# A decoder layer on one core: six weight loads in uneven parts, the last w3 in halves of its rows, and the last sums in another order

## The chip, the cores and the metric

The kernel runs on one core of a Trainium2 chip. A core has five engines with a queue of instructions each: TensorE (PE, with its weight loads shown apart as PEld), VectorE (DVE), ScalarE (ACT), GpSimd (POOL) and SyncE (SP), which here issues nearly all transfers. Sixteen DMA engines move the data between the chip's memory (HBM) and the on-chip memory of 128 partitions. Engines wait for each other and for transfers through semaphores. The metric is device microseconds of one execution, as the median of several runs.

## What is computed

The reference is one layer of a decoder for 512 tokens of width 1024, all in float32: a mixer of two kinds of attention, then a mixture of 64 experts of which each token takes two, then a final RMSNorm. The change touches the experts and the norm behind them:

```python
def expert_block(args):
    xb, e = args
    return (jax.nn.silu(xb @ w1[e]) * (xb @ w3[e])) @ w2[e]
...
x = x + hier_moe(h, w_group[l], b_group[l], w_expert[l], b_expert[l], w1[l], w3[l], w2[l])
return rms_norm(x, final_norm)
```

An expert has three matrices of 2 MB: w1 and w3 are 1024 x 512, w2 is 512 x 1024. All 64 experts' matrices are read once, 403 MB.

## The kernel before

The mixer takes the first 380 us or so. Then come the experts, in 16 batches of four (N_BATCH). Each expert has 32 places for tokens, so that a batch fills 128 rows; what doesn't fit is done after the last batch by a loop that runs as many times as a counter says (`overflow`, L1509; zero times for these inputs).

A batch runs so. The tokens of its four experts are gathered into `hsel` by matmuls with a selection matrix (g_ps, L1261). Then h1 and h3 are summed up in two accumulators (L1571): for each of eight chunks of 128 rows of the matrix, and in it for each of the four experts, one matmul of 32 columns against 512. A matmul in float32 is two instructions in the trace, so 32 matmuls per matrix stand there as 64. `swiglu` makes gg and its transpose gT, then y_ps is summed up from gT and w2 (L1608), and `combine` multiplies by the gates and adds the result to four accumulators `accs`, one for each block of 128 tokens (c_ps, L1368 and L1374). In the first batches the routing and in the fifth the row of the final norm are prepared beside it.

The weights come through a ring of eight tiles of 128 partitions x 16 KB, in three pools of 2, 4 and 2 (RING). `load_next` (L1030) takes the next entry of the list `loads`, claims the next tile and issues the transfer on SP; the tile must have been released by the matmuls that read it, so SP waits for TensorE. An entry is one expert's matrix as a whole, and the order is w1, w3, w2 with four experts each. In the last batch w2 is loaded in halves of its rows, two experts to a tile, and the second half of the rows again in column blocks (CUTS: 512, 256, 256), so that the last columns come last (`load_half`, L978).

The last batch has its own end, `last_outputs` (L1406): `values(i, chunks)` sums up y_psl for a column block, `evac(i)` copies it, `add(t, cuts)` multiplies by the gates and adds it to `accs[t]` (c_psl, L1428 and L1430), `square(t, i)` makes sums of squares on ScalarE (L1380), `final_weight` multiplies by the norm's weights on GpSimd, `final_factors` makes the reciprocal root of two blocks at a time on VectorE and GpSimd (L1388 to L1398), and `output` scales and stores. Inside it all engines run in the order of the code; in the batches before it, a scheduler orders the instructions.

Of the kernel before, what the change touches and what calls it, by code (L numbers as in the profile page):

```python
# [16 lines left out]
OP = mybir.AluOpType  # L17
# [3 lines left out]
P = 128  # L21
T = 512
NT = T // P
D = 1024
# [20 lines left out]
ANGLES_AT = 6  # L45
FORGET_AT = 13
ROUNDS = (5, 3)

CUTS = ((0, 512), (512, 768), (768, 1024))
BIG = 3e38  # L50
EPS = 1e-6
# [45 lines left out]
def kernel(ctx: ExitStack, tc: tile.TileContext, a: dict, out: bass.AP, dbg=None):  # L97
# [860 lines left out]
    loads = [[(0, m, k, e) for m, k, e in halves[n_first:n_first + 2]], [(0, m, k, e) for m, k, e in halves[n_first + 2:]]]  # L958
    for b in range(1, N_BATCH - 1):
        loads += [[(b, m, None, e)] for m in ("w1", "w3", "w2") for e in range(4)]  # L960
    loads += [[(N_BATCH - 1, m, None, e)] for m in ("w1", "w3") for e in range(4)]
    loads += [[(N_BATCH - 1, "w2", k, e + u) for u in range(2)] for k in range(2) for e in (0, 2)]
    next_places = [0] * RING[0] + [1] * RING[1] + [2] * RING[2]

    def weights(m, x, k):

        w, n = {"w1": (w1, NC), "w3": (w3, NC), "w2": (w2, 4)}[m]
        rows = w[x].rearrange("(p c) n -> p c n", c=n)
        return rows if k is None else rows[:, k * n // 2:(k + 1) * n // 2]
# [60 lines left out]
    def load_next():  # L1030

        i = len(issued) - n_first
        issued.append(i)
        t = rings[next_places[i % n_ring]].tile([P, 4096], F32, tag="ring", name=f"load{i}")
        if len(loads[i]) == 1 and loads[i][0][2] is None:
            b, m, k, e = loads[i][0]
            t = t.rearrange("p (c n) -> p c n", c=4 if m == "w2" else NC)
            nc.sync.dma_start(t, weights(m, 4 * b + e, k))  # L1038
            note(b, m, k, e, [t[:, c] for c in range(t.shape[1])])
            return  # L1040
        for u, x in enumerate(loads[i]):
            load_half(t[:, 2048 * u:2048 * u + 2048], *x)
# [335 lines left out]
    def square(t, i):  # L1378

        act.activation(gg.rearrange("p c n -> p (c n)")[:, 0:512], accs[t][:, rest_cut if i else first_cut], AF.Square,  # L1380
                       accum_out=sq4[:, t, i:i + 1])

    def final_weight(t):
        gp.tensor_tensor(outs[t][:, first_cut], accs[t][:, first_cut], fnorm[:, first_cut], op=OP.mult)
# [3 lines left out]
    def final_factors(t, n=2):  # L1388

        q, ms, r, e = (r4[:, j, t:t + n] for j in range(4))  # L1390
        v.tensor_tensor(ms, sq4[:, t:t + n, 0], sq4[:, t:t + n, 1], op=OP.add)
        v.tensor_scalar(ms, ms, 1.0 / D, EPS, op0=OP.mult, op1=OP.add)
        gp.tensor_tensor(r, ms, mhalf[:, 0:n], op=OP.pow)
        yield
        v.tensor_tensor(e, r, r, op=OP.mult)
        v.tensor_tensor(e, e, ms, op=OP.mult)
        v.tensor_scalar(e, e, -0.5, 1.5, op0=OP.mult, op1=OP.add)
        v.tensor_tensor(r, r, e, op=OP.mult)  # L1398

    def output(t):  # L1400
        r, o = r4[:, 2, t:t + 1], outs[t]
# [4 lines left out]
    def last_outputs():  # L1406

        y_ps = [o_tile(f"y_psl{i}") for i in range(2)]
        y_ps = [y_ps[0], y_ps[1][:, 0:256], s_tile("y_psl2")[:, 0:256]]
        y_sb = [ys[0], ys[1][:, 0:256], ys[1][:, 256:512]]  # L1410

        def values(i, chunks):
            for c in chunks:
                for e in range(4):
                    q = slice(32 * e, 32 * e + 32)
                    w = last[i, c][e] if c > 1 else wt[N_BATCH - 1, "w2", e][c][:, slice(*CUTS[i])]
                    pe.matmul(y_ps[i][q], gT[:, c, q], w, start=c == 0, stop=c == 3, skip_group_check=True)

        def evac(i):
            act.activation(y_sb[i], y_ps[i], AF.Copy)  # L1420

        def add(t, cuts):

            c_ps = (acc_tile if t < 2 else pt_tile)(f"c_psl{cuts[0]}_{t}")
            s = slice(CUTS[cuts[0]][0], CUTS[cuts[-1]][1])
            for i in cuts:
                a0, a1 = (x - s.start for x in CUTS[i])
                pe.matmul(c_ps[:, a0:a1], w_t[:, t], y_sb[i], start=i == cuts[0], stop=i == cuts[-1],  # L1428
                          skip_group_check=True)
            v.tensor_tensor(accs[t][:, s], c_ps, accs[t][:, s], op=OP.add)  # L1430


        for i in range(3):
            values(i, range(2))
        values(0, range(2, 4))
        evac(0)
        for t in range(2):
            add(t, (0,))
            final_weight(t)
        for t in range(2):  # L1440
            square(t, 0)
        values(1, range(2, 4))
        evac(1)
        for t in range(2, NT):
            add(t, (0,))
            final_weight(t)
        square(2, 0)
        values(2, range(2, 4))
        evac(2)
        square(3, 0)  # L1450

        f = [final_factors(t) for t in (0, 2)]
        for t in range(NT):
            add(t, (1, 2))
            square(t, 1)
            if t == 2:
                next(f[0])
        next(f[0], None)
        next(f[1])
        output(0)  # L1460
        output(1)
        next(f[1], None)
        output(2)
        output(3)

    def prepare_overflow():

        cnt = flat[7][:, 0:5 * N_EXP].rearrange("p (j e) -> p j e", j=5)
        c_n, n_blk, inc, one64, c_t = (cnt[:, j] for j in range(5))
        cnt_ps = o_tile("cnt_ps")  # L1470
        for u in range(NT):
            pe.matmul(cnt_ps[:, 0:N_EXP], ones_b, picks[:, u], start=u == 0, stop=u == NT - 1)
        v.tensor_copy(c_n, cnt_ps[:, 0:N_EXP])
        v.tensor_scalar(n_blk, c_n, float(CAP), None, op0=OP.is_gt)
        for j in range(1, 4):
            v.tensor_scalar(c_t, c_n, float(CAP + P * j), None, op0=OP.is_gt)
            v.tensor_tensor(n_blk, n_blk, c_t, op=OP.add)
        v.memset(one64, 1.0)
        v.tensor_tensor_scan(inc, one64, n_blk, 0.0, op0=OP.mult, op1=OP.add)
        v.tensor_tensor(c_t, inc, n_blk, op=OP.subtract)  # L1480
        ovs = moe.tile([P, 2, NT], F32, name="ovs")
        over = moe.tile([P, 2, NT], F32, name="over")
        val = scr[:, 0:512].rearrange("p (x t e) -> p x t e", x=2, t=NT)
        for x in range(2):
            v.tensor_tensor(val[:, x], oh[:, x], c_t[:, None, :].to_broadcast([P, NT, N_EXP]), op=OP.mult)
        v.tensor_reduce(ovs, val, axis=AX.X, op=OP.add)
        for t in range(NT):
            v.tensor_copy(exs[:, :, t], topi[:, t, 8:10])
        v.scalar_tensor_tensor(poss, exs, -float(CODE), slots, op0=OP.mult, op1=OP.add)

        v.scalar_tensor_tensor(ovs, ovs, float(P), poss, op0=OP.mult, op1=OP.add)
        v.tensor_scalar(over, poss, float(CAP), None, op0=OP.is_ge)  # L1492
        v.scalar_tensor_tensor(ovs, ovs, 1.0 - CAP, over, op0=OP.add, op1=OP.mult)
        v.tensor_scalar(ovs, ovs, -1.0, None, op0=OP.add)
        ov_row = moe.tile([1, NB_MAX + 1], F32, name="ov_row")
        ov_int = moe.tile([1, NB_MAX + 1], I32, name="ov_int")
        done = scr[0:1].rearrange("o (i e) -> o i e", e=N_EXP)
        for k in range(2):
            v.tensor_tensor(done, inc[0:1, None, :].to_broadcast([1, 16, N_EXP]),
                            iota[0:1, 16 * k:16 * k + 16, None].to_broadcast([1, 16, N_EXP]), op=OP.is_le)  # L1500
            v.tensor_reduce(ov_row[:, 16 * k:16 * k + 16], done, axis=AX.X, op=OP.add)
        v.tensor_scalar(ov_row[:, 0:NB_MAX], ov_row[:, 0:NB_MAX], float(N_EXP - 1), None, op0=OP.min)
        v.tensor_copy(ov_row[:, NB_MAX:NB_MAX + 1], inc[0:1, N_EXP - 1:N_EXP])
        v.tensor_copy(ov_int, ov_row)
        nxt = moe.tile([1, NB_MAX], I32, name="nxt")
        n_ov = nc.values_load(ov_int[0:1, NB_MAX:NB_MAX + 1], min_val=0, max_val=NB_MAX)
        return ovs, ov_int, nxt, n_ov

    def overflow(ovs, ov_int, nxt, n_ov):  # L1509
        ov_w = [u.rearrange("p (c n) -> p c n", c=2) for u in flat[7:9]]  # L1510
        ov_loads = []
        with tc.For_i(0, n_ov):
# [28 lines left out]
            for t in range(NT):  # L1541
                for i in range(2):
                    square(t, i)
                final_weight(t)
            for _ in final_factors(0, NT):
                pass
            for t in range(NT):
# [5 lines left out]
    def load_ahead(n):  # L1553
        while len(issued) - n_first < min(n, len(loads)):
            load_next()
# [3 lines left out]
    loc = slots  # L1559

    for b in range(N_BATCH):
        load_ahead(2 + 12 * b + n_ring if b else RING[0] + RING[1])
        h1, h3 = s_tile(f"h1_{b}"), s_tile(f"h3_{b}")

# [62 lines left out]
                pe.matmul(f_ps, one_row, row[:, 512 * k:512 * k + 512], start=True, stop=True)  # L1627
                act.activation(fnorm[:, 512 * k:512 * k + 512], f_ps, AF.Copy)

    overflow(*ov)  # L1630


# [24 lines left out]
```

## Time and profile before

| | us |
|---|---|
| median of 3 runs (1313.0 to 1313.3) | 1313.22 |
| the profiled execution | 1313.3 |
| its span, first to last instruction | 1311.3 |
| TensorE busy | 1126.6 |
| VectorE busy | 457.5 |
| ScalarE busy | 245.7 |
| GpSimd busy | 73.6 |

The page cuts the span in 40 slices of 32.8 us. A digit is the busy share of a slice in tenths, and below it stand the GB/s that the DMA engines moved. The mixer fills the first 11 or 12 slices, the experts the rest. PEclk, or the granted clock, is the share of TensorE's full clock of 2.4 GHz that it was given: 1.0 or 0.5 (1.2 GHz) at any moment. A busy TensorE isn't one at its peak, since matmuls are pipelined.

### The profile page before, as it was taken

The page shows a single profiled execution, that of the slowest core. Times are in us where ns is not written, and L with a number is a line of the kernel's source. Part 1 is how long each engine was busy: PE and PEld are TensorE (multiplying, and loading weights), DVE is VectorE, ACT ScalarE, POOL GpSimd, SP SyncE. Part 2 cuts the span into 40 slices and gives each one's busy share as a digit, 9 for nine tenths or more (in the row PEclk, how much of TensorE's full clock was granted, in tenths as well). Part 3 has the DMA queues.
Part 4 walks back from the last instruction along what each step waited for, and adds up shares of the span by engine and source line. Part 5 has one row for each costly group of instructions (what it writes and reads, how often), then busy time and mean ns, then how long its engine had stood idle before and what let it go on. Part 6 is the DMA issues. An engine that isn't in the chain of part 4 may idle for free.

```text
span 1311.3 us, 16877 instructions
## 1 busy us (share of the span) xinstructions
PE 1126.6 (86%) x6934; PEld 610.5 (47%) x6934; DVE 457.5 (35%) x1138; ACT 245.7 (19%) x559; POOL 73.6 (6%) x100
## 2 busy tenths in 40 slices
PE   8999999999999797978879696968878786967865
PEld 8987777878984262413233241413232331413212
DVE  7776666236263362212303121212313121211113
ACT  5665444433541000000000000000000000000003
POOL 2700000012000000000000000000000000000002
PEclk9999999999999899979989898989889998989878
DMA  5222231356989999999999999999999999999995
GB/s 185 76 66 74 78 88 55 96 146 202 347 280 417 427 427 426 428 427 428 427 426 428 427 427 426 428 426 428 428 426 427 421 428 424 428 426 427 428 421 190
DMA packets 70074, 438.92 MB, mean 335 GB/s; under 512 B 9878, under 2 KB 39594, under 8 KB 45036
## 3 DMA queue, kind: packets, MB, share of 16 engines
q1 hardware_dynamic: 69994, 437.82, 82.3%
q8 instruction: 56, 0.92, 0.3%
q14 instruction: 22, 0.18, 0.0%
q10 hardware_dynamic: 2, 0.00, 0.0%
HBM read 433.48 MB, written 2.10 MB: 332 GB/s over the span
## 4 chain that ended last, share of the span: by engine, by line
PE 63%; DMA 31%; DVE 3%; SPq 1%; issue 1%; ACT 1%; POOL 1%; DVEq 0%; POOLq 0%; ACTq 0%
DMA load<-in_w_dram 30%; PE h L1571 11%; PE y_ps L1608 9%; PE g_ps L1261 9%; PE c_ps L1368 8%; PE acc_g L322 2%; PE acc_g L323 2%; PE acc_g L324 2%; SPq L1038 1%; PE of_ps L823 1%; PE acc_wo L324 1%; PE acc_kv L433 1%; PE acc_wo L322 1%; PE acc_wo L323 1%; PE fpT_ps L805 1%
## 5 line engine op out<-in xcount | busy, mean ns | idle before, releaser
L1571 PE MATMUL h<-load,u_hi 128*32 128x512 f32 x1920 | 293.3, 671 | 88.3 <-DMA load<-in_w_dram 88.1
L1608 PE MATMUL y_ps<-load,u_hi 128*32 128x512 f32 x920 | 167.9, 680 | 53.6 <-DMA load<-in_w_dram 50.3
L1571 PEld LDWEIGHTS h<-load,u_hi 128*32 128x32 f32 x1920 | 69.6, 121 | 288.4 <-issue 155.9
L1261 PEld LDWEIGHTS g_ps<-u_hi,xc 128*128 128x128 f32 x1024 | 118.8, 194 | 24.6 <-issue 13.0
L1261 PE MATMUL g_ps<-u_hi,xc 128*128 128x128 f32 x1024 | 124.9, 281 | 0.6 <-DVE over L1492 0.6
L1374 DVE TENSOR_TENSOR u_lo<-c_ps,u_lo 128x512 f32<-128x512 f32 x84 | 58.1, 692 | 188.3 <-PE c_ps L1368 188.3
L1608 PEld LDWEIGHTS y_ps<-load,u_hi 128*32 128x32 f32 x920 | 40.5, 117 | 168.8 <-issue 89.3
L1267 DVE TENSOR_TENSOR u_hi<-g_ps,cst 128x512 f32<-128x512 f32 (+1 forms) x33 | 21.9, 667 | 278.1 <-PE h L1571 261.5
L1368 PE MATMUL c_ps<-xb,xb 128*128 128x512 f32 x240 | 116.7, 617 | 1.0 <-DVE u_lo L1371 0.8
L1355 ACT ACTIVATE xb<-h 128x512 f32<-128x512 f32 x16 | 9.6, 597 | 355.9 <-PE h L1571 355.9
L1368 PEld LDWEIGHTS c_ps<-xb,xb 128*128 128x128 f32 x240 | 37.8, 188 | 79.4 <-DVE u_lo L1374 36.8
L1343 POOL TENSOR_TENSOR xb<-xb,u_hi 128x512 f32<-128x512 f32 x16 | 20.4, 1273 | 824.8 <-DVE xb L1342 748.4
L1365 ACT ACTIVATE xb<-y_ps 128x512 f32<-128x512 f32 x30 | 17.9, 597 | 216.4 <-PE y_ps L1608 216.4
L1362 ACT ACTIVATE u_hi<-t_ps 128x512 f32<-128x512 f32 x16 | 9.6, 597 | 255.3 <-PE t_ps L1361 255.3
L322 PE MATMUL acc_g<-hT_hi,hi_g 128*128 128x512 f32 x128 | 54.2, 423 | 0.0
L1211 DVE TENSOR_SCALAR u_hi<-codes,locs,cst 128x128 f32<-128x128 f32 x60 | 21.8, 363 | 87.5 <-PE g_ps L1261 87.5
L323 PE MATMUL acc_g<-hT_lo,hi_g 128*128 128x512 f32 x128 | 50.5, 395 | 0.0
L324 PE MATMUL acc_g<-hT_hi,lo_g 128*128 128x512 f32 x128 | 50.4, 394 | 0.0
L1356 DVE TENSOR_TENSOR u_hi<-h,xb 128x512 f32<-128x512 f32 x16 | 16.5, 1033 | 90.0 <-PE h L1571 89.1
L189 DVE TENSOR_TENSOR lo_g<-raw_g,hi_g 128x1024 fp32r<-128x1024 f32 x16 | 19.6, 1226 | 36.1 <-ACT hi_g L187 36.1
L322 PE MATMUL acc_wo<-hi_wo,mT 128*128 128x256 f32 x96 | 28.7, 299 | 0.0
L324 PE MATMUL acc_wo<-hi_wo,mT 128*128 128x256 f32 x96 | 27.1, 283 | 0.1
(377 smaller groups left out, 1604.3 us busy)
## 6 DMA issues: line engine op xcount, KB each, us to landing
load<-in_w_dram SPq DMA_DIRECT2D x176, 2048.0 KB
first<-in_w_dram SPq DMA_DIRECT2D x16, 1024.0 KB
load<-in_w_dram SPq DMA_DIRECT2D x9, 1024.0 KB
raw_g<-in_w_in_dram SPq DMA_DIRECT2D x16, 512.0 KB
raw_wo<-in_w_out_dram SPq DMA_DIRECT2D x8, 512.0 KB
x_sb<-in_x_dram SPq DMA_DIRECT2D x4, 512.0 KB
raw_qs<-in_w_in_dram SPq DMA_DIRECT2D x4, 512.0 KB
raw_vf<-in_w_in_dram SPq DMA_DIRECT2D x4, 512.0 KB
```

The costliest lines, as they stand in the source:

```text
L189: defer(wait, lambda: v.tensor_tensor(lo, r, hi.bitcast(F32), op=OP.subtract))
L322: pe.matmul(o, l_hi, r_hi, start=first, stop=False, skip_group_check=True)
L323: pe.matmul(o, l_hi, r_lo, start=False, stop=False, skip_group_check=True)
L324: pe.matmul(o, l_lo, r_hi, start=False, stop=last, skip_group_check=True)
L1211: v.tensor_scalar(sel1[:, t], labels, loc[:, 0, t:t + 1], r, op0=OP.is_equal, op1=OP.mult)
L1261: pe.matmul(g_ps[k][:, c * P:(c + 1) * P], xc[t][:, 4 * k + c], sel1[:, t], start=(t, c) == (0, 0), stop=t == NT - 1, skip_group_check=True)
L1267: v.tensor_tensor(hsel[:, d], g_ps[k][:, c * P:(c + step) * P].rearrange("p (c n) -> p c n", c=step), g_ffn[:, d, None].to_broadcast([P, s ...
L1343: gp.tensor_tensor(wsel, wsel, wtmp, op=OP.add)
L1368: pe.matmul(c_ps, w_t[:, t], ys[k], start=True, stop=True)
L1374: v.tensor_tensor(d, c_ps, d, op=OP.add)
L1571: pe.matmul(o[s], hsel[:, c, s], wt[b, m, e][c], start=c == 0, stop=c == NC - 1, skip_group_check=True)
L1608: pe.matmul(y_ps[k][s], gT[:, c, s], wt[b, "w2", e][c][:, 512 * k:512 * k + 512], start=c == 0, stop=c == 3, skip_group_check=True)
```

## The change

Four things change. Line numbers move by up to nine; the words below name functions.

First, six entries of `loads`, the third expert's w1 in batches 1, 4, 6, 9, 11 and 14, are issued as three transfers: partitions 0 to 111, 112 to 119 and 120 to 127. Second, the last batch's w3 is loaded as its w2 was: the first half of the rows of experts 0 and 1, then of 2 and 3, then the second halves. Third, in `last_outputs` all four `add(t, (0,))` come before the two later column blocks of y_psl, and the mean of squares is built as one operation for each pair of blocks from a term that is made once for all four. Fourth, the counter of the overflow loop is read into the engines' registers at the start of the last batch and not in batch 1.

```diff
+UNEVEN = [(b, "w1", 2) for b in (1, 4, 6, 9, 11, 14)]
...
-    loads += [[(N_BATCH - 1, m, None, e)] for m in ("w1", "w3") for e in range(4)]
-    loads += [[(N_BATCH - 1, "w2", k, e + u) for u in range(2)] for k in range(2) for e in (0, 2)]
+    loads += [[(N_BATCH - 1, "w1", None, e)] for e in range(4)]
+
+    loads += [[(N_BATCH - 1, m, k, e + u) for u in range(2)] for m in ("w3", "w2") for k in range(2) for e in (0, 2)]
...
-            nc.sync.dma_start(t, weights(m, 4 * b + e, k))
+            src = weights(m, 4 * b + e, k)
+
+            for p0, p1 in ((0, 112), (112, 120), (120, 128)) if (b, m, e) in UNEVEN else ((0, P),):
+                nc.sync.dma_start(t[p0:p1], src[p0:p1])
...
-        v.tensor_tensor(ms, sq4[:, t:t + n, 0], sq4[:, t:t + n, 1], op=OP.add)
-        v.tensor_scalar(ms, ms, 1.0 / D, EPS, op0=OP.mult, op1=OP.add)
+        v.scalar_tensor_tensor(ms, sq4[:, t:t + n, 1], 1.0 / D, q, op0=OP.mult, op1=OP.add)
...
+    def first_sums():
+
+        v.tensor_scalar(r4[:, 0], sq4[:, :, 0], 1.0 / D, EPS, op0=OP.mult, op1=OP.add)
...
-        for t in range(2):
+        for t in range(NT):
             add(t, (0,))
             final_weight(t)
-        for t in range(2):
-            square(t, 0)
-        values(1, range(2, 4))
-        evac(1)
-        for t in range(2, NT):
-            add(t, (0,))
-            final_weight(t)
-        square(2, 0)
-        values(2, range(2, 4))
-        evac(2)
+            if t < 3:
+                square(t, 0)
+        for i in (1, 2):
+            values(i, range(2, 4))
+            evac(i)
         square(3, 0)
...
+            if t == 0:
+                first_sums()
...
+        if b == N_BATCH - 1:
+            with tc.manual_schedule(engines={E.PE, E.DVE, E.Activation, E.Pool, E.SP}):
+                n_ov = nc.values_load(ov[1][0:1, NB_MAX:NB_MAX + 1], min_val=0, max_val=NB_MAX)
```

SP's queue at the loads of batch 1, before and after. A row is a line of the kernel, the transfer, the tile that it fills and that tile's shape (partitions x elements).

```order
126 L1038 DMA load_4226<-in_w_dram 128x4096
127 L1038 DMA load_4228<-in_w_dram 128x4096
128 L1038 DMA load_4230<-in_w_dram 128x4096
129 L1038 DMA load_4232<-in_w_dram 128x4096
130 L1038 DMA load_4392<-in_w_dram 128x4096
```

```order
126 L1044 DMA load_4226<-in_w_dram 128x4096
127 L1044 DMA load_4228<-in_w_dram 128x4096
128 L1044 DMA load_4230<-in_w_dram 112x4096
129 L1044 DMA load_4230<-in_w_dram 8x4096 x2
130 L1044 DMA load_4234<-in_w_dram 128x4096
```

The third load of the batch became three transfers into the same tile, one behind the other, ahead of the fourth.

TensorE at the last batch's w3, before and after: h_15 with the higher number is the accumulator of h3. Of before four tiles take turns, one for each expert, for all eight chunks; the first rows stand here.

```order
3797 L1571 MATMUL h_15_7629<-load_7407,u_hi_3867 32x512
3798 L1571 MATMUL h_15_7630<-load_7409,u_hi_3867 32x512
3799 L1571 MATMUL h_15_7630<-load_7411,u_hi_3867 32x512
3800 L1571 MATMUL h_15_7630<-load_7413,u_hi_3867 32x512
3801 L1571 MATMUL h_15_7630<-load_7415,u_hi_3867 32x512
```

```order
3799 L1580 MATMUL h_15_7649<-load_7407,u_hi_3867 32x512 x2
3800 L1580 MATMUL h_15_7649<-load_7410,u_hi_3867 32x512 x2
3801 L1580 MATMUL h_15_7649<-load_7413,u_hi_3867 32x512 x2
3802 L1580 MATMUL h_15_7649<-load_7416,u_hi_3867 32x512 x2
3803 L1580 MATMUL h_15_7649<-load_7413,u_hi_3867 32x512 x2
```

The first four chunks now read only the first two tiles (7407 and 7410, the first halves of all four experts' rows), and the last four only the other two; before, each chunk read all four tiles.

TensorE at the end, before and after: y_psl are the three column blocks of the last product, c_psl their sums with the gates.

```order
3844 L1417 MATMUL y_psl_7720<-load_7621,u_hi_3868 32x512 x8
3845 L1428 MATMUL c_psl_0_7756<-xb_3060,xb_3061 128x512
3846 L1428 MATMUL c_psl_1_7760<-xb_3060,xb_3061 128x512
3847 L1417 MATMUL y_psl_7721<-load_7624,u_hi_3868 32x256 x8
3848 L1428 MATMUL c_psl_2_7775<-xb_3060,xb_3061 128x512
3849 L1428 MATMUL c_psl_3_7779<-xb_3060,xb_3061 128x512
3850 L1417 MATMUL y_psl_7722<-load_7624,u_hi_3868 32x256 x8
```

```order
3823 L1426 MATMUL y_psl_7739<-load_7640,u_hi_3868 32x512 x8
3824 L1437 MATMUL c_psl_0_7775<-xb_3060,xb_3061 128x512
3825 L1437 MATMUL c_psl_1_7780<-xb_3060,xb_3061 128x512
3826 L1437 MATMUL c_psl_2_7785<-xb_3060,xb_3061 128x512
3827 L1437 MATMUL c_psl_3_7790<-xb_3060,xb_3061 128x512
3828 L1426 MATMUL y_psl_7740<-load_7643,u_hi_3868 32x256 x8
3829 L1426 MATMUL y_psl_7741<-load_7643,u_hi_3868 32x256 x8
```

The second column block moved behind the third and fourth sums of the first, and stands next to the third block.

## Rows read from the trace of the kernel before

**Rows 1.** The page: busy time of engines; DMA share and GB/s by slice

```profile
PE 1126.6 (86%) x6934; PEld 610.5 (47%) x6934; DVE 457.5 (35%) x1138; ACT 245.7 (19%) x559; POOL 73.6 (6%) x100
...
DMA  5222231356989999999999999999999999999995
GB/s 185 76 66 74 78 88 55 96 146 202 347 280 417 427 427 426 428 427 428 427 426 428 427 427 426 428 426 428 428 426 427 421 428 424 428 426 427 428 421 190
```

**Rows 2.** Chain that ended last: start us, us, what; its shortest and longest load wait

```profile
498.94 22.78 DMA load<-in_w_dram
...
1242.46 29.92 DMA load<-in_w_dram
```

**Rows 3.** One stretch: its length, engines' busy us (instructions), granted clock, DMA share, GB/s

```profile
400.00:1260.00 860.00, 703.06 (x4182) 272.76 (x4178) 210.97 (x499) 44.56 (x77) 20.37 (x16) 0.92 1.01 427
```

**Rows 4.** The page's DMA parts: queue, packets, MB, share; an issue and its size

```profile
q8 instruction: 56, 0.92, 0.3%
...
load<-in_w_dram SPq DMA_DIRECT2D x176, 2048.0 KB
```

**Rows 5.** Stretches of 1 us at the end of the last loads, columns as above

```profile
1288.00:1289.00 1.00, 1.00 (x16) 0.33 (x12) 0.00 (x0) 0.00 (x0) 0.00 (x0) 1.00 0.87 291
1289.00:1290.00 1.00, 0.83 (x8) 0.00 (x0) 0.00 (x0) 0.10 (x1) 0.00 (x0) 1.00 0.56 194
1290.00:1291.00 1.00, 0.45 (x1) 0.30 (x2) 0.00 (x0) 0.50 (x1) 0.00 (x0) 1.00 0.46 159
1291.00:1292.00 1.00, 1.00 (x4) 0.38 (x2) 0.29 (x1) 0.00 (x0) 0.00 (x0) 1.00 0.24 83
1292.00:1293.00 1.00, 1.00 (x14) 0.36 (x16) 0.83 (x2) 0.56 (x2) 0.46 (x1) 1.00 0.06 19
```

**Rows 6.** Stretches of 1 us during a load of w_proj_fox and two of w_proj_swa

```profile
257.00:258.00 1.00, 1.00 (x6) 0.79 (x5) 0.74 (x1) 0.23 (x1) 0.00 (x0) 1.00 0.72 253
...
298.00:299.00 1.00, 1.00 (x6) 0.79 (x5) 0.33 (x2) 0.00 (x0) 0.00 (x0) 1.00 1.19 209
299.00:300.00 1.00, 1.00 (x6) 0.82 (x5) 0.67 (x1) 0.00 (x0) 0.26 (x1) 1.00 1.13 219
```

**Rows 7.** Timeline of the issues of these loads: start us, us, queue, line, transfer

```profile
254.92 0.37 SPq L174 DMA_DIRECT2D raw_pf<-in_w_proj_fox_dram  x1
...
295.23 1.27 SPq L174 DMA_DIRECT2D raw_ps<-in_w_proj_swa_dram  x2
```

**Rows 8.** Timeline of TensorE at the last w3; in brackets idle time before, and what ended it

```profile
1267.61 1.91 PE L1571 MATMUL h<-load,u_hi 128*32 128x512 f32 x2 [3.97 <-DMA load<-in_w_dram]
...
1272.42 9.52 PE L1571 MATMUL h<-load,u_hi 128*32 128x512 f32 x58 [2.91 <-DMA load<-in_w_dram]
...
1274.13 0.20 PEld L1571 LDWEIGHTS h<-load,u_hi 128*32 128x32 f32 x4 [0.66 <-issue]
...
1278.35 0.12 PEld L1571 LDWEIGHTS h<-load,u_hi 128*32 128x32 f32 x4 [0.31 <-issue]
```

**Rows 9.** Two stretches of 5 us during the last w3, columns as in rows 3

```profile
1272.00:1277.00 5.00, 4.58 (x24) 1.18 (x28) 0.00 (x0) 0.00 (x0) 0.00 (x0) 0.50 1.01 417
1277.00:1282.00 5.00, 4.94 (x38) 1.06 (x30) 0.00 (x0) 0.00 (x0) 0.00 (x0) 0.96 1.02 390
```

**Rows 10.** Timeline of the end: last group of y_psl, a sum, and two small operations

```profile
1295.38 1.07 PE L1417 MATMUL y_psl<-load,u_hi 128*32 128x256 f32 x16
...
1298.55 0.69 DVE L1430 TENSOR_TENSOR u_lo<-c_psl,u_lo 128x512 f32<-128x512 f32 x1 [0.17 <-PE c_psl L1428]
...
1300.09 0.16 DVE L1391 TENSOR_TENSOR r<-sq 128x2 f32<-128x2 f32 x1
...
1300.29 0.17 DVE L1392 TENSOR_SCALAR r<-r 128x2 f32<-128x2 f32 x1
```

**Rows 11.** SP's waits: queue, line, for whom; us in total, times, longest

```profile
SPq L1038 <- PE h L1571: 497.4, 37, 22.4
...
SPq L994 <- PE h L1571: 26.4, 3, 17.9
```

More of the change, by code (lines that the diff above doesn't have):

```diff
@@ L1505, in prepare_overflow @@
         nxt = moe.tile([1, NB_MAX], I32, name="nxt")
-        n_ov = nc.values_load(ov_int[0:1, NB_MAX:NB_MAX + 1], min_val=0, max_val=NB_MAX)
-        return ovs, ov_int, nxt, n_ov
+        return ovs, ov_int, nxt
     def overflow(ovs, ov_int, nxt, n_ov):
@@ L1544, in overflow @@
                 final_weight(t)
+            first_sums()
             for _ in final_factors(0, NT):
@@ L1628 @@
                 act.activation(fnorm[:, 512 * k:512 * k + 512], f_ps, AF.Copy)
-    overflow(*ov)
+    overflow(*ov, n_ov)
 _INS = ["x", "positions", "attn_norm", "w_in", "b_forget", "b_gate", "attn_sinks", "w_proj_fox",
```

## The prediction, made before the changed kernel had run

> **What bounds the kernel now.** I read the busy table first, then the slices, then the chain of waits, and last the two places that the change touches. TensorE is busy 86% of the span, but from the twelfth slice on the DMA row stands at 9 and the bytes at 417 to 430 GB/s with hardly a break [rows 1]. Over the 860 us from 400 to 1260 the sixteen DMA engines are busy all the time (share 1.01) and move 427 GB/s [rows 3]. The chain confirms that this stage is the loads' own: each batch of four experts ends in a wait of 22 to 30 us for a weight load before TensorE goes on [rows 2]. So a microsecond of TensorE inside a batch is worth nothing, and a microsecond of a DMA engine counts, if that engine is one that finishes last. Only behind the last load does TensorE's own work set the end.
>
> A load is 2048 KB [rows 4], 128 rows of 16 KB; at 427 GB/s it takes 4.9 us, and an engine moves a row of 16 KB in 0.61 us (427/16 = 26.7 GB/s). The engines don't stop together: the share falls from 0.87 through 0.46 to 0.06 between 1288 and 1293 [rows 5]. Summed, they stop 2.8 us before 1293 on average, half of them by about 1290, so half have some 3 us to spare. A cause is at hand: 56 instruction fetches of 16 KB ride on the same engines [rows 4], and they need not fall evenly.
>
> **The change, part by part.** The profiled execution took 1313.3 us with a span of 1311.3; the median of the three runs is 1313.22, so the sum is made on 1313.3 and needs no correction.
>
> *Six loads in 112, 8 and 8 rows.* The bytes stay the same. With a row to an engine, 112 rows are seven for each of sixteen, and each piece of 8 is one row for eight engines. If both pieces go to the same eight, these move nine rows for such a load and the others seven: over six loads 6 x 0.61 = 3.7 us more on eight engines and 3.7 us less on the others. If the eight are the early half, this evens out what the share row shows.
>
> The price of a piece is what the trace doesn't show. Its lower end is 0.61 us, a row at the usual rate. But few partitions are slow in this trace: the load of w_proj_fox, which fills 128 partitions, moves 253 GB/s at a share of 0.72, which is 351 GB/s of busy engines, while the loads of w_proj_swa, of 64 partitions each, run with all engines busy at 209 and 219 GB/s [rows 6, 7]. The engines are not short of work there, each byte only takes 351/214 = 1.64 times as long. If a piece of 8 partitions is no worse than that, its row takes 0.61 x 1.64 = 1.0 us. If the rate goes on falling with the partitions, 8 of 128 get 1/16 of 427 GB/s, and the 128 KB of a piece take 4.9 us. I take 2.2 us, the middle of 1.0 and 4.9 by ratio: the step from 128 to 64 cost less than in proportion, and eight partitions go much further down than 64. Twelve pieces then cost 12 x (2.2 - 0.61) = 19.1 us on the engines that carry them. The whole range is 0 (lower end) to 12 x 4.3 = 51.5 us. An engine that waits in a piece gets nothing back later, since what is queued behind it, the next load, runs at the full rate anyway.
>
> The SBUF page of the Trainium skill ("SBUF — State Buffer", Door 1: The DMA port swizzle) has a rule that speaks against this part. It says that four neighbouring partitions share one of sixteen ports, and gives 27.6 GB/s for partitions 0 to 3. By it partitions 112 to 119 lie on two ports, a piece takes an estimated 2.4 us, and the sum below would be 1332.8. The trace agrees in direction (64 partitions at 0.61 of the rate); eight partitions no row here shows. Its DMA page ("DMA: Bandwidth & Descriptors", Why a DMA increments its semaphore by 16 and not by 1) would send an 8-partition copy to the eight lowest-numbered engines; no row shows engine numbers.
>
> Twelve more issues on SP cost nothing: SP stands 497 us waiting for TensorE before such loads [rows 11]. That wait is the cover; without it they would cost about 0.4 us each.
>
> *The last w3 in halves of its rows.* Today TensorE does a few matmuls of w3 early, the last 2 of these at 1267.6, and 58 of 64 only after 1272.42, when the fourth expert's load is in: 9.5 us, its first 5 us at a granted clock of 0.50 and the rest near 1.0 [rows 8, 9]. In the new order the first half of the rows of all four experts is multiplied before the last piece lands, and 28 of 64 stay. In the trace 4 weight loads with their matmuls follow each other in 0.86 us at the low level (1.2 GHz) and in 0.43 at the high one (2.4) [rows 8], so 28 take 3.0 to 6.0 us, and the gain ahead of the SwiGLU is 3.5 to 6.5 us. It can't all reach the end: the last bytes of w2 land shortly before 1293 [rows 5], and today the last 16 matmuls on them start at 1295.38 [rows 10]. So at most 2.4 us come out of the wait, then the landing is late next. I book 2.4.
>
> *The order of the last sums.* All four first sums stand before the last two groups of y_psl, which then run back to back. That fits the landing just named and costs nothing while TensorE waits there; ACT takes three squares before the second copy, covered by the same wait. On VectorE two operations of 0.16 and 0.17 us become one, twice [rows 10]; one of the two places lies on the path, with a bit of the other: 0.3 us. The added operation on all four sums falls in the gap of 0.17 us that VectorE has ahead of its sums [rows 10].
>
> *The register load of the overflow count* goes from batch 1, where SP waited for it, to the last batch. There it stands ahead of a wait of up to 17.9 us for h [rows 11], so it is hidden; where it stood it cost nothing, since the engines were full (share 1.01 [rows 3]). Zero. In batches 4, 6, 9, 11 and 14 TensorE also takes one group of matmuls a little later; the wait for loads hides that.
>
> **Sum.** Pieces +19.1, extra rows on the eight engines +3.7, their spare time -3.0, the end -2.4 - 0.3: +17.1 us, 1330.4. With a piece at 1.0 us it is +2.7 (1316), at 4.9 us +49.5 (1363).
>
> **The rivals.**
> *Pieces at the usual rate.* The eight engines are spread over 3 us, so they may not meet at the same partitions, and the rows are large. Then the loads end 0 to 2.2 us earlier (2.2 is perfect evenness, the sum of the shares in [rows 5]); with 1.5 us and the end's 2.7 the time is 1309.1. This is the case on the other side, and it decides for faster as soon as a piece stays under about 0.8 us, since 12 x 0.2 = 2.4 is about what the evening and the end give. Against it stands the row of 64 partitions.
> *The pieces meet the late half.* At the usual rate, but on engines that finish last: +3.7 - 2.7, 1314.3, within what can be told. Or the rows are halved with no gain at the end: 1312 to 1313.
>
> **How the numbers follow.** Slow pieces 0.56, by the only rows that show few partitions. Usual rate 0.36, because no row has pieces of 16 KB rows on eight engines. The late half or no gain 0.08. The range goes from 1306, a bit below the fast rival, to 1346, which takes a piece at up to 3.6 us; slow pieces alone would be 1316 to 1363. A change of 0.2% (2.6 us) is about what a measurement of this kernel tells from none. Faster by more than that 0.38 (the fast rival and a little of the third), within 0.06, slower 0.56.
>
> **What would show it.** If the pieces are slow, the bytes in 20 us around each of the six loads fall from 427 GB/s by a twentieth or more, waits of TensorE for loads grow in batches 1, 4, 6, 9, 11 and 14, and the first multiplication of w3's last batch comes 15 us or more later. If they aren't, the steady stage stays at 427 GB/s, and the DMA share before the last landing stays near 1 and then drops within 1 or 2 us. In both cases fewer than 30 matmuls of w3 should follow the last w3 landing, and the last group of y_psl should start right at w2's landing. I am wrong if the six batches show no more wait than the others, or if the end doesn't close up by 2 us.

## The result: 4.45% slower

The changed kernel took 1372.16 us in the median (1367.8 to 1374.9), the kernel before 1313.0 beside it: a ratio of 1.0445, 95% interval 1.0431 to 1.0459. That is 59 us more, where the prediction said 17. The direction was right; the time lies above the range.

The page of the changed kernel, the parts that answer to [rows 1]:

```profile
PE 1141.1 (83%) x6934; PEld 613.2 (45%) x6934; DVE 457.2 (33%) x1137; ACT 246.1 (18%) x559; POOL 73.5 (5%) x100
...
DMA  6223232375899999999999999999999999999994
GB/s 186 63 63 94 72 85 61 93 232 196 311 370 345 427 425 427 426 346 427 428 426 307 428 426 427 397 330 421 427 420 331 421 418 387 425 377 365 424 409 160
```

TensorE runs as many instructions as before (6934). The DMA row stands at 9 from the thirteenth slice to the last but one, as before, but in six places the bytes fall (345, 346, 307, 330, 331 and 365 GB/s at their lowest): the engines don't run out of work, their work takes longer. Stretches of 20 us around the third of these places, batch 6 (columns as in rows 3; the last two are the DMA share and GB/s):

```profile
700.00:720.00 20.00, 16.90 (x125) 5.04 (x125) 6.48 (x20) 1.69 (x3) 1.28 (x1) 0.91 1.03 426
720.00:740.00 20.00, 18.04 (x87) 10.13 (x85) 6.91 (x12) 1.19 (x2) 0.00 (x0) 1.00 0.99 222
740.00:760.00 20.00, 11.03 (x65) 2.55 (x66) 0.00 (x0) 0.60 (x1) 0.00 (x0) 0.79 1.01 428
```

For 20 us everything moves at half speed, with a share of 0.99, and then all is well again. Two whole loads' bytes pass in this time, though only one load is in parts. In stretches of 1 us:

```profile
718.00:719.00 1.00, 1.00 (x16) 0.36 (x9) 0.00 (x0) 0.00 (x0) 0.00 (x0) 1.00 0.81 344
719.00:720.00 1.00, 1.00 (x10) 0.23 (x3) 0.00 (x0) 0.00 (x0) 0.00 (x0) 1.00 1.62 426
720.00:721.00 1.00, 1.00 (x3) 0.11 (x1) 0.00 (x0) 0.60 (x1) 0.00 (x0) 1.00 0.86 180
721.00:722.00 1.00, 1.00 (x3) 0.49 (x3) 0.00 (x0) 0.60 (x1) 0.00 (x0) 1.00 0.87 180
```

A row counts a packet whole in the stretch in which it starts, so a single one is coarse (the shares of 1.62 and 0.86), but from 720 on the rate is half of what it was. The engines, however, are some microseconds apart from each other, as [rows 5] show at the end of the kernel before. Had only those slowed that had reached the load in parts, the bytes would have fallen over 4 or 5 us.

The trace also has records of the single packets and of the time at which each engine's share of a transfer lands, which no view lists. By them the first engine comes to the 112 partitions at 719.38, the last at 729.62, and the last leaves them at 738.19. The 16 KB packets of all sixteen engines take 0.61 us until about 719.6 and some 1.2 us from then on; they get shorter as the last engines leave, and are at 0.61 again from about 739.5. So all sixteen slow down when three of them have come to the 112 partitions.

The chain of waits shows the same places as load waits longer than any of before (its longest was 29.92 us, [rows 2]; elsewhere in this chain none is over 31.52); four of them:

```profile
709.70 35.28 DMA load<-in_w_dram
...
893.67 39.55 DMA load<-in_w_dram
...
1021.41 40.60 DMA load<-in_w_dram
...
1237.40 35.24 DMA load<-in_w_dram
```

Where the time went, summed up over stretches: six of 24 to 40 us around the six loads, each its length x (1 - rate/427), give 6.4, 6.5, 9.8, 8.3, 7.7 and 8.9 us, 47.7 together. Two of them and two others answer to it in these rows (batch 6, batch 14; then two places where the share itself drops, so that engines stood without work):

```profile
718.00:742.00 24.00, 21.19 (x106) 10.86 (x98) 6.91 (x12) 1.19 (x2) 0.00 (x0) 0.98 1.01 252
...
1222.00:1250.00 28.00, 23.54 (x126) 11.54 (x121) 5.53 (x8) 1.19 (x2) 0.00 (x0) 1.00 1.01 291
...
860.00:880.00 20.00, 19.72 (x139) 10.27 (x138) 3.60 (x8) 0.60 (x1) 0.00 (x0) 1.00 0.92 378
1120.00:1140.00 20.00, 16.76 (x132) 9.54 (x130) 1.39 (x4) 0.60 (x1) 0.00 (x0) 1.00 0.88 359
```

These two places give 20 x (1 - 378/427) = 2.3 and 3.2 us. Some 6 us are left. At the end the engines stop over a longer time than in [rows 5]: the share falls to 0.35 some 14 us ahead of the last bytes. By the landing records one engine is 7 us behind the fifteen others there; for the loads of the last w3 the last engine lands some 8.9 us behind the mean of the sixteen, and 3.5 in the kernel before. That is about 5 of the 6 us.

```profile
1339.00:1340.00 1.00, 0.75 (x7) 0.17 (x5) 0.00 (x0) 0.95 (x2) 0.00 (x0) 1.00 0.35 125
...
1353.00:1354.00 1.00, 1.00 (x3) 0.19 (x1) 0.83 (x2) 0.77 (x3) 1.00 (x2) 1.00 0.04 14
```

### The profile page after: what moved, and what is told of

Same layout as the page of the kernel before. It is cut to its first block, busy times and chain, and to the rows that moved or that the text cites. A ratio compares the mean times of both kernels' runs of the same rounds, so it can differ in the third digit from the quotient of the medians.

```text
span 1370.9 us, 16898 instructions
## 1 busy us (share of the span) xinstructions
PE 1141.1 (83%) x6934; PEld 613.2 (45%) x6934; DVE 457.2 (33%) x1137; ACT 246.1 (18%) x559; POOL 73.5 (5%) x100
## 4 chain that ended last, share of the span: by engine, by line
DMA 48%; PE 47%; DVE 2%; SPq 1%; issue 1%; POOL 1%; ACT 1%; DVEq 0%; POOLq 0%; ACTq 0%
DMA load<-in_w_dram 47%; PE h L1580 10%; PE y_ps L1617 5%; PE g_ps L1267 3%; PE acc_g L324 2%; PE c_ps L1374 2%; PE acc_g L325 2%; PE acc_g L326 2%; PE acc_kv L435 1%; SPq L1044 1%; PE of_ps L825 1%; PE acc_wo L326 1%; PE acc_wo L324 1%; PE acc_wo L325 1%; PE fpT_ps L807 1%
## 5 line engine op out<-in xcount | busy, mean ns | idle before, releaser
L1580 PE MATMUL h<-load,u_hi 128*32 128x512 f32 x1920 | 307.0, 680 | 128.9 <-DMA load<-in_w_dram 128.9
```

Source lines behind the costliest of these rows:

```text
L1580: pe.matmul(o[s], hsel[:, c, s], wt[b, m, e][c], start=c == 0, stop=c == NC - 1, skip_group_check=True)
```

## The experiments

Three theories stood against each other. **A**: the pieces of 8 partitions are slow, as the prediction had it. **B**: the transfer of 112 partitions already makes engines get in each other's way, and all sixteen are held up while any is in it. **C**: three transfers cost more than one, whatever their shape. All edits below are against the changed kernel unless it is said otherwise.

### No load in parts

```diff
-UNEVEN = [(b, "w1", 2) for b in (1, 4, 6, 9, 11, 14)]
+UNEVEN = []
```

> The changed kernel with no load in parts; the other three edits stay. Three theories on the 59 us that the change cost. A: each piece of 8 partitions holds its engines for some 5 us. B: the transfer of 112 partitions itself sends its rows so that engines get in each other's way, and all transfers run at half speed from the moment the first engine enters such a load until the last one leaves it (in the profile of after the bytes fall to 222 GB/s over 720:740 with the share at 0.99). C: three transfers in place of one cost it, whatever their shape. All three expect the loss gone here and the end shorter by the 2.4 + 0.3 us of the prediction: 1310.5. If the three other edits bring nothing, 1313.

Measured: 1311.58 us against 1312.37, ratio 0.9994 (0.9985 to 1.0003). The whole loss goes with the six loads. The three other edits together bring 0.8 us, inside the uncertainty, and not 2.7.

### The same parts by columns

```diff
-            for p0, p1 in ((0, 112), (112, 120), (120, 128)) if (b, m, e) in UNEVEN else ((0, P),):
-                nc.sync.dma_start(t[p0:p1], src[p0:p1])
+            if (b, m, e) in UNEVEN:
+                for s in (np.s_[:, 0:7], np.s_[:, 7, 0:256], np.s_[:, 7, 256:512]):
+                    nc.sync.dma_start(t[s], src[s])
+            else:
+                nc.sync.dma_start(t, src)
```

> The same six loads in three parts of 1792, 128 and 128 KB, but cut by columns: each part goes to all 128 partitions. C expects the loss to stay, about 1372. A and B expect it gone: within 2 us of the kernel with no load in parts, no slice under 420 GB/s in the middle of the experts.

Measured: 1312.77, ratio 1.0001 (0.9991 to 1.001), 1.2 us above the kernel with no load in parts. The page's row of bytes:

```profile
GB/s 183 78 66 74 77 87 57 95 147 202 345 280 416 428 426 426 428 426 427 425 429 424 428 427 426 428 426 427 426 429 423 428 426 416 428 425 426 427 418 209
```

From the thirteenth slice to the last but one no slice is under 416, near the 420 that was asked. Three transfers in place of one, two of them of 128 KB, cost nothing that can be told from the spread of the runs, and C falls. The split by partitions is what costs.

### 112 and 16 partitions

```diff
-            for p0, p1 in ((0, 112), (112, 120), (120, 128)) if (b, m, e) in UNEVEN else ((0, P),):
+            for p0, p1 in ((0, 112), (112, 128)) if (b, m, e) in UNEVEN else ((0, P),):
```

> The same six loads in two parts, 112 and 16 partitions; no piece of 8 is left, each engine gets seven rows and then one. A expects half the loss or less (six pieces where there were twelve): 1340 or under. B expects about the same as with 112, 8 and 8: 1365 to 1375, and the half-speed stretch to begin before the piece of 16 is reached.

Measured: 1364.53, ratio 1.0383 (1.0367 to 1.0399), just below the 1365 that B gave and far from A's 1340. A stretch around batch 6's load:

```profile
716.00:740.00 24.00, 22.05 (x114) 11.09 (x106) 6.92 (x12) 1.20 (x2) 0.00 (x0) 1.00 1.01 264
```

The stretch stays, a little shallower (264 GB/s in 24 us against 252). Two pieces of 8 in place of one of 16 cost 7.6 us in six loads by the medians, with 7 and 9 us between the lowest and highest runs of the two, so this difference is rough; 53 us remain without any piece of 8.

### Half a load on 112 partitions, nothing behind it

```diff
...
+                nc.sync.dma_start(t[:, 0:4], src[:, 0:4])
+                nc.sync.dma_start(t[0:112, 4:8], src[0:112, 4:8])
...
```

> Leaves work out: of the six loads the first four of a row's eight parts go to 128 partitions (TensorE multiplies these twice), the other four parts to partitions 0 to 111 in one transfer that nobody reads. No piece of 8 or 16 is left; 0.125 MB less per load, 1.8 us in all. Theory B, the 112 rows are enough: the same place at half speed from the first engine that enters (2.1 us of work in it, and the lead of some 2 to 6 us): 4 to 8 us per load, 1335 to 1358. If it takes the small pieces behind the 112: 1310.

Measured: 1339.25, ratio 1.0195 (1.0173 to 1.0217). Against 1311.58 less the 1.8 us of missing bytes that is 29.5 us lost, 4.9 per load, with half the bytes and no small piece at all.

```profile
716.00:728.00 12.00, 10.70 (x34) 3.95 (x33) 5.53 (x8) 0.25 (x1) 0.00 (x0) 1.00 1.03 251
```

So the 112 partitions are enough, in B's range and near its lower end.

### The six loads one behind the other

```diff
-UNEVEN = [(b, "w1", 2) for b in (1, 4, 6, 9, 11, 14)]
+UNEVEN = [(9, "w1", e) for e in range(4)] + [(9, "w3", e) for e in range(2)]
```

> The six uneven loads stand one behind the other in batch 9 (four w1 and two w3) and not one each in six batches. A and C: each costs the same wherever it stands, 1370. B: the half-speed stretch lasts from the first engine that enters the first of them to the last that leaves the last, so the lead of the first engine over the last (some 5 us there) is paid once and not six times: 6 x 4.9 + 5 = 34 us lost, 1345 (1340 to 1352).

Measured: 1352.05, ratio 1.0304 (1.0288 to 1.032): 40 us lost in place of 60. Three stretches, before, over and behind the six loads:

```profile
860.00:870.00 10.00, 8.56 (x64) 2.77 (x57) 3.53 (x8) 1.09 (x2) 0.54 (x1) 0.94 1.00 424
...
870.00:950.00 80.00, 43.09 (x208) 15.66 (x204) 9.87 (x24) 1.79 (x3) 0.74 (x1) 0.76 1.01 242
...
950.00:960.00 10.00, 6.40 (x26) 1.37 (x30) 0.00 (x0) 0.00 (x0) 0.00 (x0) 0.50 1.01 431
```

One slow stretch of some 75 us, inside 80 us at a mean of 242 GB/s: 80 x (1 - 242/427) = 34.7 us. The price is not one per load. A part of it, (60.6 - 40.5) / 5 = 4.0 us each time, is paid for entering and leaving, as B has it: the stretch begins with the first engine and ends with the last. The measured time lies at the upper edge of B's bounds; 5.8 of the 40 us lie outside this stretch and stay unexplained.

### Four pieces of 8: each engine at its own partitions, or four engines at neighbours

One of the two lines for `p` stands in each kernel.

```diff
...
+                nc.sync.dma_start(t[:, 0:4], src[:, 0:4])
+                for i in range(4):
+                    p = slice(i, 32, 4)              # pieces_own
+                    p = slice(8 * i, 8 * i + 8)      # pieces_crowded
+                    nc.sync.dma_start(t[p, 4:8], src[p, 4:8])
...
```

> Leaves work out: of the six loads only the first four of a row's eight parts are loaded on 128 partitions (TensorE multiplies these twice), and then 32 partitions' other four parts in four pieces of 8 partitions, which nobody reads: partitions 0, 4, .. 28, then 1, 5, .. 29, and so on. 0.75 MB less per load, which frees 1.2 us on eight engines and 2.4 on the others. The idea of shared ports (four neighbouring partitions have one, as the Trainium skill says in SBUF — State Buffer, Door 1: The DMA port swizzle): every engine of a piece has a port for itself, so nothing is lost: 1297 to 1304, no slice of the page under 400 GB/s. A, a piece of 8 partitions is slow as such: 24 pieces of half a row at 2.5 us, 1340 or more.

> Leaves the same work out; the same 32 partitions in four pieces of 8 neighbours: 0 to 7, 8 to 15, 16 to 23, 24 to 31. Same bytes, same number of instructions in the same order. Shared ports, where only the engines of the piece wait: four engines on a port, 3.7 us more per load on eight engines, 1319 to 1326. Shared ports, where the crowded ones hold up all sixteen (B): from the first engine that enters to the last that leaves, some 6 us of work at a quarter to half of the speed: 6 to 18 us per load, 1335 to 1400. A: as with pieces_own, 1340 or more, both alike.

Measured: 1304.45 (0.9937, 0.9922 to 0.9952) and 1318.02 (1.0036, 1.0023 to 1.0049). The first lies half a microsecond above what shared ports gave for it (1297 to 1304), the second one below (1319 to 1326). Same bytes, same partitions, same instructions in the same order, and 13.6 us between them. A stretch of 7 us that holds the pieces of batch 6, first of the one, then of the other:

```profile
703.00:710.00 7.00, 6.98 (x16) 2.17 (x15) 3.47 (x6) 1.19 (x2) 0.00 (x0) 1.00 1.01 421
```

```profile
709.00:716.00 7.00, 6.98 (x20) 2.00 (x18) 5.17 (x8) 0.00 (x0) 0.00 (x0) 1.00 1.02 311
```

A piece of 8 partitions is not slow as such: with steps of four partitions it moves at full rate. With 8 neighbours the rate falls to 311 GB/s for 7 us, 1.9 us per load by this row, 2.26 by the times. The rule of the Trainium skill ("SBUF — State Buffer", Door 1: The DMA port swizzle) that four neighbouring partitions share a port agrees with both.

The time of the crowded pieces is that of "only the engines of the piece wait" (1319), and not my price for all sixteen. Yet the records of the single packets, which no view lists, show all sixteen engines slower here: their 16 KB packets, 0.61 us before, take 0.7 to 1.2 us for some 7 us. All were held up, but weakly and briefly; my price for it was too high. In the changed kernel the same records go from 0.61 to 1.2 us and more on all sixteen engines within about 0.2 us of each other, at 719.6.

### Two halves of 64 partitions: neighbours, or even and odd

```diff
-            for p0, p1 in ((0, 112), (112, 120), (120, 128)) if (b, m, e) in UNEVEN else ((0, P),):
+            for p0, p1 in ((0, 64), (64, 128)) if (b, m, e) in UNEVEN else ((0, P),):                # parts_64_64
+            for p in (slice(0, P, 2), slice(1, P, 2)) if (b, m, e) in UNEVEN else (slice(0, P),):  # even_odd
...
```

> The same six loads in two halves of 64 neighbouring partitions. If sixteen engines get the rows in order, four each, two engines write to the same four neighbours' port all the time, though 64 is as even as it could be: like 112 and 16, 1355 to 1372. If only a number that isn't a power of two, or a slice that doesn't begin at a port, disturbs: 1312.

> The same six loads in two halves, the even and the odd partitions, so that each half reaches all sixteen ports. If an engine is chosen by the partition (as it looks for whole loads), each engine keeps its port: 1312. If the rows are handed out in order, engine e gets partitions 8e, 8e+2, 8e+4, 8e+6, and two engines share a port at any moment while other ports stand idle: 1355 to 1372 again. If it only matters that all ports are within reach of the transfer: 1312.

Measured: 1358.93 (1.038, 1.0336 to 1.0424) and 1312.23 (1.0001, 0.9992 to 1.0011). A stretch of the first, and the page's bytes of the second:

```profile
718.00:740.00 22.00, 19.95 (x102) 10.63 (x97) 6.92 (x12) 1.19 (x2) 0.00 (x0) 1.00 1.01 284
```

```profile
GB/s 184 78 66 74 77 87 57 96 145 204 344 283 416 427 427 421 428 427 428 428 426 428 426 428 427 427 428 427 427 427 427 428 426 423 429 425 427 427 417 207
```

Even parts of neighbours cost nearly as much as 112 and 16; even and odd partitions cost nothing. My guess for rows that are simply handed out in order, that the even partitions would crowd too, did not come true. Nor do the groups of four that a transfer reaches decide it: 112 neighbours take in 28 of the 32 and 64 neighbours 16, at nearly the same cost. What fits every run is that in a whole load and in every second partition each engine meets partitions that no other engine writes at that moment, and in a run of 112 or 64 neighbours it doesn't. This is argued from the times: which engine gets which rows of the 112 was not seen. A rival also stays untested. A weight's row and its partition go together in all these loads, so each pair of runs changes the rows read from HBM as well as the partitions written, and no run moves one without the other. That the crowd is at the partitions, and not at the rows of HBM, rests on the agreement with the rule on ports.

### The last w3 in halves alone, the order of the last sums alone

The first is the kernel before with the two lines of `loads` from the change; the second is the changed kernel with whole loads everywhere.

> The kernel before with one edit: the last w3 in halves of its rows. The three edits beside the loads together brought 0.8 us (1311.58 against 1312.37) where the prediction booked 2.7. By the prediction this edit carries 2.4 of them: 1310.0. If the last w2 landing sets the end anyway: 1312.4, with the first matmuls of w3 earlier but the last group of y_psl at the same time.

> The changed kernel with whole loads everywhere, the w3 of the last batch too: what is left is the order of the last sums and the register load. By the prediction it carries 0.3 us: 1312.1. If the order of the sums costs something, because the four first sums now stand ahead of the last two groups of y_psl: 1313 or more, with those groups later.

Measured: 1312.6 (0.9999, 0.999 to 1.0008) and 1311.95 (0.9994, 0.9985 to 1.0003). Neither can be told from no change. TensorE at the end with both edits and no load in parts (timeline: start us, us, instructions; in brackets idle time before, and what ended it):

```profile
1272.16 5.03 PE L1580 MATMUL h<-load,u_hi 128*32 128x512 f32 x26 [1.46 <-DMA load<-in_w_dram]
...
1279.72 1.06 PE L1426 MATMUL y_psl<-load,u_hi 128*32 128x512 f32 x6 [0.25 <-ACT u_hi L1368]
1282.20 4.49 PE L1426 MATMUL y_psl<-load,u_hi 128*32 128x512 f32 x50 [1.42 <-DMA load<-in_w_dram]
1287.52 1.06 PE L1426 MATMUL y_psl<-load,u_hi 128*32 128x512 f32 x8 [0.83 <-DMA load<-in_w_dram]
1289.30 3.70 PE L1437 MATMUL c_psl<-xb,xb 128*128 128x512 f32 x8 [0.72 <-ACT xb L1429]
1292.93 1.93 PE L1426 MATMUL y_psl<-load,u_hi 128*32 128x256 f32 x32
1294.79 3.86 PE L1437 MATMUL c_psl<-xb,xb 128*128 128x256 f32 x16
```

and in the kernel before, the rows that answer to it:

```profile
1284.47 5.37 PE L1417 MATMUL y_psl<-load,u_hi 128*32 128x512 f32 x64 [0.25 <-ACT u_hi L1362]
1290.55 1.98 PE L1428 MATMUL c_psl<-xb,xb 128*128 128x512 f32 x4 [0.72 <-ACT xb L1420]
...
1296.38 3.86 PE L1428 MATMUL c_psl<-xb,xb 128*128 128x256 f32 x16
```

TensorE comes to y_psl 4.75 us earlier (1279.72 against 1284.47), within the 3.5 to 6.5 that were forecast ahead of the SwiGLU. But then it waits twice for w2, until 1287.52 for the last load of the first column block, and the first sums start only 1.25 us earlier (1289.30 against 1290.55). From there its own work, 3.70 + 1.93 us, leads to the last sums, which start 1.6 us earlier in this execution; the medians say 0.8.

## Why the prediction was right and wrong

**What bounds the kernel** was right: the loads. The kernel follows the bytes, and TensorE's time in the batches didn't matter. One reading was a slice early: the DMA row stands at 9 from the thirteenth slice on, not the twelfth, at 416 to 428 GB/s.

**The step that failed** is in the first sentences on the six loads: "The bytes stay the same. With a row to an engine, 112 rows are seven for each of sixteen". That gave the transfer of 112 partitions the usual rate, and all the cost to the two pieces behind it; the sum has no term for the 112 rows. The runs show the reverse: 112 partitions cost 29.5 us in six halves of a load without any piece, and 53 us in the six with a piece of 16 behind. The row that could have told stood in the text. [Rows 6] show loads of 64 partitions at 209 and 219 GB/s with all engines busy, and I took it as a price for small slices of partitions. By the two runs with halves of 64 it is a price for slices of neighbours, and 112 is one. The 1.64 was also misread: the first rate was divided by its share, 0.72, and the other two were not, though their shares are 1.19 and 1.13. Divided alike, they give 176 and 194 GB/s and a factor near 1.9, which moves the sum by some 2 us.

**The price of a piece** was too high rather than too low. In the changed kernel the row of a second piece lands 1.3 us behind the first piece's on the same engine (mean of 40 pairs in the landing records, 0.9 to 2.0), where the sum had 2.2, and in that stretch a row of a whole load takes 1.2 as well. Four crowded pieces of half a row cost 2.26 us more than four that are not crowded, 0.57 each; twice that for a whole row is an estimate of 1.1 us more, where the sum had 2.2 - 0.61 = 1.6. Twelve pieces make some 8 us by the first and 14 by the second, and not 19.1, and the 112 rows beside them are missing from the sum. That the time moved the way that was forecast is thus in part luck, and so is the upper end, 51.5 us, that comes near the whole loss.

**Who waits** was the second error. The sum charged the engines that carry a piece. In the trace all engines slow down together, at once, and the stretch lasts about as long as any of them is in such a load. That the next load "runs at the full rate anyway" fell with it. That makes the distance between the first engine and the last a part of the price, six times over; [rows 5] had that distance, and I used it only as spare time.

**The spare time of the eight engines**, -3.0, did not show itself. With uncrowded pieces the eight engines that carry them save 1.2 us per load, 7.3 in all by the rows of 0.61 us, the others 14.7. The gain was 7.1 (1311.58 to 1304.45), that of the eight. Had they had 3 us to spare, it would have been near 10. The landing records agree. With the uncrowded pieces the last engine of all carries them in four of the six loads, and in the changed kernel in all six, so the rival *the pieces meet the late half* named the right engines.

**The end** was right in kind and too large: 2.4 + 0.3 booked, 0.8 measured (between 2.0 gained and 0.4 lost by the interval). "The landing is late next" was right; the wrong landing was named. The last bytes, near 1293, were not the next limit but those of the first column block at about 1287.5, behind which 5.4 us follow, nearly all of them TensorE's work, before the last groups of y_psl.

**Signs.** As foretold for slow transfers, the bytes fell by more than a twentieth around the six loads and the waits grew in their batches. As foretold for both cases, fewer than 30 matmuls follow the last w3 landing (26 at 1333.37, where [rows 8] have 58), and the last groups of y_psl start at about the last bytes of w2:

```profile
1333.37 3.62 PE L1580 MATMUL h<-load,u_hi 128*32 128x512 f32 x26 [1.46 <-DMA load<-in_w_dram]
...
1354.07 1.93 PE L1426 MATMUL y_psl<-load,u_hi 128*32 128x256 f32 x32
```

They start there without a wait for a load, straight behind the first sums, so this sign came true for another reason than the one given. One of the two signs of being wrong came too: the end closed up by 0.8 us (1311.58 against 1312.37), and not by 2. The issues on SP cost nothing, which the run with parts by columns shows apart.

**The rivals.** "Pieces at the usual rate", 1309.1 with a chance of 0.36, was wrong in this kernel. It is right for pieces that step over neighbours, which the change doesn't have. The 0.56 for slow pieces was on the right side with the wrong piece.

## What to carry to other kernels

In a stream of loads that keeps all engines busy, as here, cut a load by columns, each part to all 128 partitions, or into every second partition, but not into runs of neighbouring partitions: 64 and 64 cost 7.9 us per load of 4.9 us here, even and odd nothing. A DMA share of 1.0 doesn't mean full speed; read the bytes beside it, and where they halve, look for a transfer whose partitions differ from those around it. To price such a transfer, count the distance between the first and the last engine too, since one misplaced transfer slows what runs beside it.

## What was unexpected in the hardware

- One transfer of 112 partitions in a stream of whole ones takes all engines from 427 GB/s to about half (222 over the next 20 us) within a microsecond, by the packet records also those that are still in the load ahead, when three of the sixteen have come to it. Why they all slow is not settled: engines that wait for a shared port could hold up a path that all use, but no run separates that path.
- Eight engines move pieces of 8 partitions at the full rate if the partitions are four apart (421 GB/s in all), and crowd if they are neighbours (311).
- Transfers of 64 partitions run at the full rate if they take every second partition: 1312.23 us, against 1358.93 for neighbours.
- The engines stay apart for hundreds of microseconds: in the kernel before, the sixteen shares of a load land within 2.3 us near 440 and within some 6.4 near 1260. Six disturbing loads in a row cost 40 us, six scattered ones 60.
- What remains open: the rows of a 112-partition transfer by engine, whether the rows of HBM have a part in it, the two places with a share of 0.92 and 0.88, and 5.8 us of the six loads in a row.
